# Down projection on one core: side blocks of weights loaded later in the lead, and the next sum's first operand rounded ahead of the current sum's second pass

## The chip, the cores and the metric

The kernel runs on one core of one Trainium2 chip, in one launch. The metric is device time in microseconds (us). Three runs of the kernel before gave 2108.65, 2109.05 and 2110.7 us; their median is 2109.05 us. One more execution was profiled: it took 2109.45 us, and its span, from the first to the last instruction of the program, is 2107.5 us.

## The reference, cut to what matters

Two layers of a decoder trunk in float32, on x of 512 tokens by 1024. Each layer has two feed-forward modules (with a mixer of recurrence and attention between them), so there are four feed-forward modules in all:

```
def swiglu(h, w_gate, w_up, w_down):
    return (jax.nn.silu(h @ w_gate) * (h @ w_up)) @ w_down     # D = 1024, D_FF = 2816

x = x + 0.5 * rms_norm(swiglu(rms_norm(x, gn[0]), w_ffn1_gate[l], w_ffn1_up[l], w_ffn1_down[l]), gn[1])
...
x = x + 0.5 * rms_norm(swiglu(rms_norm(x, gn[4]), w_ffn2_gate[l], w_ffn2_up[l], w_ffn2_down[l]), gn[5])
```

The change touches the last product of each feed-forward module, the activations (512 x 2816) by `w_down` (2816 x 1024): the down projection.

## The kernel before, in words

**Every product is three matmuls.** A float32 operand is split into a rounded part (hi, type float32r) and what is left (lo). `mm3` (L211) multiplies hi by hi, hi by lo and lo by hi. So each operand costs ScalarE one copy for hi and VectorE one subtraction for lo (`split`, L230); in `split_dma` (L241) ScalarE makes hi and minus the source (lines L408 and L409 of the profile), and GpSimd issues a DMA that adds the source (L410). For weights the copies are L274 and L322.

**Engines and order.** TensorE's order is the order of the code. The instructions of the other engines are ordered when the program is built, by a scheduler that follows the code where nothing is in the way; `pin` keeps an instruction behind the one written before it on its engine. Once built, each engine runs its own queue in order, and waits on semaphores.

**Tiles.** `big()` (L52) gives a 2 KB per partition tile of the pool tag `s`, which has 61 rooms (`SLOTS`). Tiles of one tag get their rooms in the order in which the code first writes them, and each takes the free room that has been free longest; the writer then waits on the chip until the last reader of the room's old tile is done. Weights arrive in four `w32` tiles; their hi and lo parts live in six `whi` and six `wlo` tiles.

**The down projection (`down`, `fast=True`).** The activations are 22 blocks `src[k]` of 128 features by 512 tokens. The first 12 go through a product of seven quarter products (`quarters`), the last 10 through ordinary products. It runs in this order:

1. The **lead**: five units j = 6 to 10 (`both(j, 0)`), each with the blocks k = 2j and 2j+1, four token blocks and three matmuls each: 24 matmuls of 512 columns. The blocks 16 to 21 are rounded into `part` just ahead of it, 12 tiles of `s`; the tiles of a unit come free when the unit is done.
2. During the lead `Late.sums` (L615) makes the operands of the quarter products, one call for each k = 0 to 5, two calls after each of the first three units. A call splits the first half of `src[k]` into `x1[k]` (ScalarE copy L398, VectorE L399), builds sums `s` and `t` (VectorE L456, L457, L459, L460), and splits `t` by `split_dma` into `x37` (L408, L409, L410). It takes five tiles of `s`.
3. The seven products in the order p1, p3, p7, p2, p6, p4, p5 (`ORDER`), each of 36 matmuls: six k, two token blocks, three matmuls. Each uses three blocks of weights, q = 0 to 2, made in `Stream.quarter`. p1 uses the raw blocks; p3 and p5 the side blocks `b22`; p7 the side blocks `b12` after `b22` has been added to them (L255).
4. The second half of the ordinary products, and the norm.

**Order of the weights.** `Stream` holds the blocks of weights in the order in which TensorE uses them. A used block leads to the splits of the blocks ahead (`ahead`, with `most` of them), and a split block lets `load` issue the next DMA on SyncE's queue (SP; L233 and L236). In `load`, when the last raw block of p1 has been asked for, the 24 DMAs of the side blocks follow on the same queue at once (L245): two tiles of `s` for each of three q, for `b22` and for `b12`, 12 tiles in all. This is ahead of the lead in the code. After `whi` of p1's block q = 0, which is written in the third unit, those of q = 1 and 2 are written in the fourth unit, that is behind all six sums, and they are pinned there.

Of the kernel before, what the change touches and what calls it, by code (L numbers as in the profile page):

```python
# [8 lines left out]
F32R = mybir.dt.float32r  # L9
# [6 lines left out]
P = 128  # L16
D = 1024
S = 512
# [14 lines left out]
    first=0.0, spread=2300.0, squares=1700.0, lay=34500.0, laid=770.0, normed=7600.0, final=2600.0,  # L33
# [11 lines left out]
def trunk(ctx: ExitStack, tc: tile.TileContext, xin, wall, gains, lbT, hgain, sinks, c_dist, c_mask, c_ident, out):  # L45
    nc = tc.nc
    cp = ctx.enter_context(tc.tile_pool(name="cp", bufs=1))
    sb = ctx.enter_context(tc.tile_pool(name="sb", bufs=1))
    ps = ctx.enter_context(tc.tile_pool(name="ps", bufs=1, space=PSUM))
# [8 lines left out]
    def nm(s):  # L58
        seq[0] += 1
        return f"{s}_{seq[0]}"  # L60

    def big(dt=F32, shape=None):
        return sb.tile(shape or [P, S], dt, tag="s", name=nm("s"), bufs=SLOTS)
# [15 lines left out]
    class Order:  # L79
        def __init__(self):  # L80
            self.t = 0.0
            self.rest = 0.0
            self.cos = []
# [60 lines left out]
    pin = tc.keep_in_program_order  # L144
# [10 lines left out]
    class Stream:  # L155
        def __init__(self):
            self.n, self.wall = 0, 0
            self.items = []
            self.raw, self.dma = {}, 0
            self.done, self.flight = 0, 0  # L160
            self.cur, self.c = 0, 0
            self.src = {}
            self.pinned = False
            self.most = AHEAD
            self.side, self.freed = {}, 0

        def plain(self, n, kind="u"):
            self.items += [Item(kind, self.n + i) for i in range(n)]
# [23 lines left out]
        def rows(self, kt, fast):  # L192

            u0 = self.wall

            def pieces(j, h):
                b = [(4 * h + i) * kt + 2 * j for i in range(4)]
                return [(slice(i * 2 * P, (i + 1) * 2 * P), wall[u0 + n // 8][:, n % 8 * P : (n % 8 + 2) * P]) for i, n in enumerate(b)]  # L200

            def unit(j, h):
                c = 2 * j * P
                self.src[self.n] = [(None, wall[u0 + 4 * h : u0 + 4 * h + 4, :, c : c + 2 * P].rearrange("u p c -> p u c"))] if kt == 8 else pieces(j, h)
                self.plain(1)

            lead = range(SEVEN // 2 if fast else 0, kt // 2)
            for j in lead:
                unit(j, 0)
            if fast:  # L210

                u, n = self.n, SEVEN // 4
                for q in range(n):
                    self.src[u + q] = pieces(q, 0)
                    self.src[u + n + q] = pieces(n + q, 0)
                self.side[u + n - 1] = [pieces(n + q, 1) for q in range(n)], [pieces(q, 1) for q in range(n)]
                for k in ORDER:
                    for q in range(n):
                        it = Item(k, u + q + (n if k in ("p2", "p4") else 0), 4)
                        it.base, it.q = u, q  # L220
                        self.items.append(it)
                self.n += 2 * n
            for j in lead:
                unit(j, 1)
            self.wall = u0 + kt

        def load(self, upto):
            while self.dma < min(upto, self.n):
                w = sb.tile([P, D], F32, tag="w32", name=nm("w32"), bufs=W32)
                u = self.dma  # L230
                if isinstance(self.src[u], list):
                    for c, a in self.src[u]:
                        nc.sync.dma_start(w.rearrange("p (m c) -> p m c", m=4) if c is None else w[:, c], a)  # L233
                else:
                    for c in (slice(0, D // 2), slice(D // 2, D)) if u == 0 else (slice(0, D),):
                        nc.sync.dma_start(w[:, c], wall[self.src[u]][:, c])  # L236
                self.raw[u] = w
                self.dma += 1
                if u in self.side:
                    self.b22, self.b12, self.t2 = [], [], []  # L240
                    for b, side in zip((self.b22, self.b12), self.side[u]):  # L241
                        for ps in side:
                            v = [big(), big()]
                            for c, a in ps:
                                nc.sync.dma_start(v[c.start // S][:, c.start % S : c.start % S + 2 * P], a)  # L245
                            b.append(v)

        def quarter(self, it):

# [42 lines left out]
        def split(self):  # L292
            it = self.items[self.done]
            if it.kind[0] == "p":
                return self.quarter(it)
            u, last = it.u, it.kind in "uvd"
            self.load(u + (1 if it.kind in "uv" else 2))
            it.hi = sb.tile([P, D], F32R, tag="whi", name=nm("whi"), bufs=WS)
            it.lo = sb.tile([P, D], F32R, tag="wlo", name=nm("wlo"), bufs=WS)
            w, h = self.raw[u], (slice(0, D // 2), slice(D // 2, D))  # L300
            cols = (slice(0, D),)
            if it.kind == "u" and u == 0:
                cols = h
            if it.kind in "bcd":
                v = self.raw[u + 1]
            if it.kind == "b":

                self.t13 = sb.tile([P, D], F32, tag="tt", name=nm("tt"), bufs=2)
                pin(nc.vector.tensor_tensor(self.t13[:, h[0]], w[:, h[0]], v[:, h[0]], op=ALU.add))
                pin(nc.vector.tensor_tensor(self.t13[:, h[1]], v[:, h[0]], v[:, h[1]], op=ALU.add))  # L310
                w = self.t13
            elif it.kind == "c":

                t = sb.tile([P, D], F32, tag="tt", name=nm("tt"), bufs=2)
                pin(nc.vector.tensor_tensor(t[:, h[0]], self.t13[:, h[0]], v[:, h[1]], op=ALU.add))
                pin(nc.vector.tensor_tensor(t[:, h[1]], t[:, h[0]], w[:, h[1]], op=ALU.add))  # L316
                w = t
            elif it.kind == "d":
                w = v
                cols = h[1:]  # L320
            for c in cols:
                i = nc.scalar.copy(it.hi[:, c], w[:, c])  # L322
                if u < 3 or self.pinned:
                    pin(i)
                if it.kind in "vad":
                    nc.scalar.mul(it.lo[:, c], w[:, c], -1.0)  # L326
                    nc.gpsimd.dma_start(it.lo[:, c].bitcast(F32), w[:, c], accum_op=ALU.add)  # L327
                else:
                    nc.vector.tensor_tensor(it.lo[:, c], w[:, c], it.hi[:, c].bitcast(F32), op=ALU.subtract)  # L329
            self.done += 1  # L330
            self.flight += 1
            if last:
                nu = u + (1 if it.kind in "uv" else 2)
                for i in range(u, nu):
                    self.raw.pop(i)
                    self.freed += 1
                self.load(self.freed + W32)
# [38 lines left out]
    ws = Stream()  # L376
# [37 lines left out]
    HALF = (slice(0, S // 2), slice(S // 2, S))  # L414
# [51 lines left out]
    def pair_split(v, how=split):  # L466
        return how(v, to=(big(F32R, [P, 2, S // 2]), big(F32R, [P, 2, S // 2])))
# [139 lines left out]
    class Late(Quarters):  # L607
# [5 lines left out]


        def sums(self):  # L615
            k = len(self.x1)
            a = [self.src[i][:, c] for i in (k, k + self.n) for c in HALF]
            x = big(F32R, [P, 2, S // 2])
            self.x1.append(split(a[0], to=(x[:, 0, :], x[:, 1, :]), hold=pin))
            s, t = quarter_sums(a[0], a[2], a[1], a[3], True)  # L620
            self.s.append(s)
            self.x37.append(pair_split(t, split_dma))
            self.src[k] = ()

        def rest(self):
            for k in range(self.n, 2 * self.n):
                self.src[k] = split_dma(self.src[k])
# [9 lines left out]
    def down(src, kt, l, n, nxt, fast):  # L637
# [47 lines left out]

        if fast:
            late = Late(src)
            ws.pinned = True
            for k in range(2 * js[0] + EARLY, kt):
                part[k] = split(src[k], hold=pin)  # L690
            for i, j in enumerate(js):
                ws.most = (3, 2, 2, 3, 3)[i]
                both(j, 0)
                while len(late.x1) < min(late.n, 2 * i + 2):
                    late.sums()
                for k in (2 * j, 2 * j + 1):
                    part.pop(k, None)
            ws.pinned = False
            more = quarters(late, y, lambda: (ready(kt), fetch()))
        else:  # L700
            for j in js:
                ready(2 * j + 2 + EARLY)
                both(j, 0)
            fetch()
# [762 lines left out]
```

## Time and profile before

| what | value |
|---|---|
| median of three runs | 2109.05 us |
| the profiled execution, its own time | 2109.45 us |
| its span | 2107.5 us |
| TensorE matmul busy | 2087.7 us, 99% |
| VectorE busy | 1588.2 us, 75% |
| ScalarE busy | 1180.9 us, 56% |
| DMA, mean over the span | 149 GB/s |
| share of the granted TensorE clock, mean | 0.996 |

Times inside the trace are counted from the start of the span. The first feed-forward module has its lead at about 241 to 268 us; the other three have the same work at about 938, 1285 and 1980 us. In a row of the timeline stand the start, the length, the engine, the line, the operation with its tiles (out<-in), the shape, how often, and in brackets the idle time of the engine just before and what ended it. The lines that carry the argument are shown in the prediction.

### The profile page before, as it was taken

To read this page: it belongs to the slowest core of one execution; us is meant where nothing else is said; L and a number is where in the kernel's file an instruction comes from. 1 tells how busy PE (TensorE), PEld (TensorE's weight loads), DVE (VectorE), ACT (ScalarE), POOL (GpSimd) and SP (SyncE) were. 2 spreads that over 40 slices of the span, in tenths; PEclk is the share of its full clock that TensorE was granted. 3 is DMA by queue.
4 is the path that set the end of the run, shared out by engine and by line. 5 is a ranking of instruction groups with operands and counts; after the bars stand their busy time and mean duration, and the time that the engine had idled before them with its cause. 6 is when DMAs were issued, how large, how long until landed. Compare 5 with 4: busy or idle time off the path is not lost. (4 is left out here: it accounts for less than half of the span.)

```text
span 2107.5 us, 35599 instructions
## 1 busy us (share of the span) xinstructions
PE 2087.7 (99%) x13501; PEld 1870.3 (89%) x13501; DVE 1588.2 (75%) x2801; ACT 1180.9 (56%) x2035; POOL 203.1 (10%) x244
## 2 busy tenths in 40 slices
PE   9999999999999999999999999999999999999998
PEld 8899978887888999997899998888778989999977
DVE  5877779766786777786987777887686758777777
ACT  6555566456454555556555555754654545555564
POOL 0011120000000011112001111100000000111120
PEclk9999999999999999999999999999999999999999
DMA  8577865312236357776637777652122563677863
GB/s 247 151 182 182 215 126 194 111 61 71 71 101 203 127 122 182 183 198 150 189 112 175 182 182 194 140 193 93 51 81 60 136 194 101 163 181 182 213 135 108
DMA packets 156139, 313.07 MB, mean 149 GB/s; under 512 B 17888, under 2 KB 75712, under 8 KB 155968
## 3 DMA queue, kind: packets, MB, share of 16 engines
q1 hardware_dynamic: 122416, 228.16, 32.9%
q0 software_dynamic: 33408, 82.59, 22.7%
q8 instruction: 106, 1.74, 0.3%
q14 instruction: 65, 0.53, 0.1%
q10 hardware_dynamic: 144, 0.05, 0.0%
HBM read 213.43 MB, written 14.73 MB: 108 GB/s over the span
## 5 line engine op out<-in xcount | busy, mean ns | idle before, releaser
L114 PE MATMUL acc<-s,whi 128*128 128x256 f32 (+1 forms) x4952 | 1059.9, 311 | 0.6 <-ACT whi L322 0.4
L114 PEld LDWEIGHTS acc<-s,whi 128*128 128x128 f32 x4952 | 808.0, 191 | 52.4 <-issue 4.0
L114 PE MATMUL acc<-s,wlo 128*128 128x256 f32 (+1 forms) x2476 | 766.5, 310 | 0.1
L114 PEld LDWEIGHTS acc<-s,wlo 128*128 128x128 f32 x2476 | 472.6, 191 | 24.9 <-DVE wlo L329 0.4
L114 PE MATMUL acc<-whi,s 128*128 128x512 f32 x1344 | 442.3, 396 | 9.8 <-ACT whi L274 9.8
L322 ACT CAST whi<-w 128x512 fp32r<-128x512 f32 (+1 forms) x325 | 299.6, 942 | 163.0 <-PE acc L114 107.5
L322 ACT CAST whi<-tt 128x1024 fp32r<-128x1024 f32 x154 | 161.4, 1048 | 327.2 <-DVE tt L316 188.5
L114 PEld LDWEIGHTS acc<-whi,s 128*128 128x128 f32 x1344 | 254.4, 189 | 69.4 <-ACT whi L274 11.5
L329 DVE TENSOR_TENSOR wlo<-w,whi 128x1024 fp32r<-128x1024 f32 (+1 forms) x165 | 199.8, 1215 | 89.6 <-ACT whi L322 88.9
L114 PE MATMUL acc<-wlo,s 128*128 128x512 f32 x672 | 264.4, 393 | 1.2 <-DVE wlo L277 1.2
L329 DVE TENSOR_TENSOR wlo<-tt,whi 128x1024 fp32r<-128x1024 f32 x154 | 188.1, 1222 | 99.8 <-ACT whi L322 99.5
L327 POOL DMA_DIRECT2D wlo<-w x160 | 138.2, 864 | 1231.2 <-ACT wlo L326 715.5
L114 PE MATMUL aux<-s,whi 128*128 128x256 f32 (+1 forms) x1248 | 230.4, 285 | 0.0
L114 PEld LDWEIGHTS aux<-s,whi 128*128 128x128 f32 x1248 | 195.2, 192 | 1.1 <-issue 0.5
L114 PE MATMUL aux<-s,wlo 128*128 128x256 f32 (+1 forms) x624 | 177.5, 284 | 0.0
L114 PE MATMUL aux<-whi,s 128*128 128x512 f32 x480 | 159.2, 390 | 0.0
L114 PEld LDWEIGHTS acc<-wlo,s 128*128 128x128 f32 x672 | 127.5, 190 | 27.5 <-DVE wlo L277 2.5
L326 ACT ACTIVATE wlo<-w 128x1024 fp32r<-128x1024 f32 (+1 forms) x160 | 129.8, 844 | 0.0
L114 PEld LDWEIGHTS aux<-s,wlo 128*128 128x128 f32 x624 | 119.8, 192 | 0.3
L114 PEld LDWEIGHTS aux<-whi,s 128*128 128x128 f32 x480 | 90.1, 188 | 18.6
L911 DVE SCALAR_TENSOR_TENSOR s<-m 128x512 f32<-128x512 f32 x69 | 47.8, 693 | 76.2 <-ACT m L910 75.7
L398 ACT CAST s<-s 128x512 fp32r<-128x512 f32 (+1 forms) x148 | 78.2, 563 | 47.2 <-DVE s L457 43.6
(185 smaller groups left out, 2374.4 us busy)
## 6 DMA issues: line engine op xcount, KB each, us to landing
w<-wall SPq DMA_DIRECT2D x267, 512.0 KB, 3.8
wlo<-w POOLq DMA_DIRECT2D x83, 512.0 KB, 5.5
w<-wall SPq DMA_DIRECT2D x256, 128.0 KB, 3.1
wlo<-w POOLq DMA_DIRECT2D x77, 256.0 KB, 3.3
s<-s POOLq DMA_DIRECT2D x72, 256.0 KB, 4.8
x_d<-s SPq DMA_DIRECT2D x48, 256.0 KB, 2.1
s<-wall SPq DMA_DIRECT2D x96, 128.0 KB, 3.5
s<-x_d SPq DMA_DIRECT2D x48, 256.0 KB, 5.3
```

The lines of the kernel that those rows point to most:

```text
L114: nc.tensor.matmul(o, lhsT, rhs, start=start, stop=stop)
L322: i = nc.scalar.copy(it.hi[:, c], w[:, c])
L326: nc.scalar.mul(it.lo[:, c], w[:, c], -1.0)
L327: nc.gpsimd.dma_start(it.lo[:, c].bitcast(F32), w[:, c], accum_op=ALU.add)
L329: nc.vector.tensor_tensor(it.lo[:, c], w[:, c], it.hi[:, c].bitcast(F32), op=ALU.subtract)
L398: hold(nc.scalar.copy(hi, src))
L911: nc.vector.scalar_tensor_tensor(z, m[:, 0:2, :], -1.0, m[:, 2:4, :], op0=ALU.mult, op1=ALU.mult)
```

## The change

The side blocks are no longer loaded in `load`. A new function `aside` issues the same DMAs into the same kind of tiles; `down` calls it for `b22` after the third unit of the lead and its sums (`i == 2`), and for `b12` after the fourth unit (`i == 3`). `Late.sums` is turned: the split of the first operand moves into a function `first`; the call for k makes its sums, then calls `first(k + 1)`, and then splits `t`. Instructions and DMAs are the same in number, size and kind; only their places differ.

```
     def rows(self, kt, fast):
-                self.side[u + n - 1] = [pieces(n + q, 1) for q in range(n)], [pieces(q, 1) for q in range(n)]
+                self.side.append(([pieces(n + q, 1) for q in range(n)], [pieces(q, 1) for q in range(n)]))
     def load(self, upto):
-                if u in self.side:
-                    self.b22, self.b12, self.t2 = [], [], []
-                    for b, side in zip((self.b22, self.b12), self.side[u]):
-                        for ps in side:
-                            v = [big(), big()]
-                            for c, a in ps:
-                                nc.sync.dma_start(v[c.start // S][:, c.start % S : c.start % S + 2 * P], a)
-                            b.append(v)
+        def aside(self, pieces):
+            b = []
+            for ps in pieces:
+                v = [big(), big()]
+                for c, a in ps:
+                    nc.sync.dma_start(v[c.start // S][:, c.start % S : c.start % S + 2 * P], a)
+                b.append(v)
+            return b
     def sums(self):                                   # class Late
-            k = len(self.x1)
+            k = len(self.s)
             a = [self.src[i][:, c] for i in (k, k + self.n) for c in HALF]
-            x = big(F32R, [P, 2, S // 2])
-            self.x1.append(split(a[0], to=(x[:, 0, :], x[:, 1, :]), hold=pin))
+            if not k:
+                self.first(0)
             s, t = quarter_sums(a[0], a[2], a[1], a[3], True)
             self.s.append(s)
+            if k + 1 < self.n:
+                self.first(k + 1)
             self.x37.append(pair_split(t, split_dma))
             self.src[k] = ()
+        def first(self, k):
+            x = big(F32R, [P, 2, S // 2])
+            self.x1.append(split(self.src[k][:, HALF[0]], to=(x[:, 0, :], x[:, 1, :]), hold=pin))
     def down(...):
             late = Late(src)
+            b22, b12 = ws.side.pop(0)
...
                 both(j, 0)
-                while len(late.x1) < min(late.n, 2 * i + 2):
+                while len(late.s) < min(late.n, 2 * i + 2):
                     late.sums()
+                if i == 2:
+                    ws.b22 = ws.aside(b22)
+                elif i == 3:
+                    ws.b12, ws.t2 = ws.aside(b12), []
```

More of the change, by code (lines that the diff above doesn't have):

```diff
@@ L164, in __init__ @@
             self.most = AHEAD
-            self.side, self.freed = {}, 0
+            self.side, self.freed = [], 0
         def plain(self, n, kind="u"):
```

## The prediction

> **What bounds the kernel now.** The page comes first:
>
> ```profile
> span 2107.5 us, 35599 instructions
> ...
> PE 2087.7 (99%) x13501; PEld 1870.3 (89%) x13501; DVE 1588.2 (75%) x2801; ACT 1180.9 (56%) x2035; POOL 203.1 (10%) x244
> ```
>
> TensorE (PE) is busy for all but 19.8 us. The change removes no matmul, so it can only win what TensorE waits. The waits of TensorE alone:
>
> ```profile
> PE acc L114 <- ACT whi L274: 9.8, 4, 2.4
> ...
> PE acc L114 <- DVE wlo L277: 1.2, 4, 0.3
> ```
>
> L274 and L277 make hi and lo of the weights of the quarter products. TensorE waits for them once in each of the four feed-forward modules: 2.45 us for hi, 0.3 for lo. The timeline of TensorE at the first of these places:
>
> ```profile
> 268.25 0.39 PE L114 MATMUL acc<-whi,s 128*128 128x512 f32 x1
> ...
> 270.52 0.39 PE L114 MATMUL acc<-wlo,s 128*128 128x512 f32 x1
> 270.75 0.39 PE L114 MATMUL acc<-whi,s 128*128 128x512 f32 x1
> 273.58 0.50 PE L114 MATMUL acc<-whi,s 128*128 128x512 f32 x1 [2.44 <-ACT whi L274]
> 274.39 0.50 PE L114 MATMUL acc<-wlo,s 128*128 128x512 f32 x1 [0.31 <-DVE wlo L277]
> 274.73 0.85 PE L114 MATMUL acc<-whi,s 128*128 128x512 f32 x2
> 275.37 0.63 PE L114 MATMUL acc<-wlo,s 128*128 128x512 f32 x1
> 275.80 1.05 PE L114 MATMUL acc<-whi,s 128*128 128x512 f32 x2
> 276.65 0.63 PE L114 MATMUL acc<-wlo,s 128*128 128x512 f32 x1
> 277.08 1.05 PE L114 MATMUL acc<-whi,s 128*128 128x512 f32 x2
> 277.93 0.60 PE L114 MATMUL acc<-wlo,s 128*128 128x512 f32 x1
> 278.36 0.64 PE L114 MATMUL acc<-whi,s 128*128 128x512 f32 x2
> 278.84 0.40 PE L114 MATMUL acc<-wlo,s 128*128 128x512 f32 x1
> ```
>
> p1's first matmul starts at 268.25, where the lead ends, and its twelfth, the last of block q = 0, at 270.75: a step is 2.50 / 11 = 0.227 us. The place costs more than the idle time in brackets. From 270.75 to 274.73 there are 3 steps, worth 0.68 us, and they take 3.98: 3.30 us lost. From 274.73 to 278.84 there are 11 steps, worth 2.50, and they take 4.11: 1.61 us more, with no wait at all. The windows say why; they are the 10 us ahead of the first place, and 5 us behind each of the four:
>
> ```profile
> 260.00:270.00 10.00, 10.00 (x46) 8.29 (x45) 5.25 (x13) 3.99 (x9) 1.72 (x2) 1.00 0.64 146
> ...
> 273.50:278.50 5.00, 4.61 (x12) 3.43 (x13) 5.00 (x10) 4.19 (x9) 0.15 (x1) 0.66 0.30 52
> 970.00:975.00 5.00, 4.63 (x12) 3.46 (x13) 5.00 (x10) 4.16 (x9) 0.13 (x1) 0.66 0.31 54
> 1317.00:1322.00 5.00, 4.69 (x20) 3.65 (x20) 5.00 (x9) 3.93 (x8) 0.00 (x0) 1.00 0.32 56
> 2012.00:2017.00 5.00, 4.69 (x14) 3.50 (x15) 5.00 (x10) 3.99 (x8) 0.86 (x1) 0.66 0.30 52
> ```
>
> The column after the brackets is the granted clock: 1.00 ahead, 0.66 behind three of the four waits. So three places cost 3.30 + 1.61 = 4.91 us and the third, where the clock stays, 3.30: together 3 x 4.91 + 3.30 = **18.0 us**.
>
> **Why hi comes late.** A unit is 24 x 0.227 = 5.45 us; the lead ends at 268.25, so its units 3, 4 and 5 end at 257.4, 262.8 and 268.25. VectorE and ScalarE in that time:
>
> ```profile
> 256.67 0.43 DVE L456 TENSOR_TENSOR s<-s,s 128x256 f32<-128x256 f32 x1 [1.18 <-PE aux L114]
> 257.01 0.42 DVE L460 TENSOR_TENSOR s<-s 128x256 f32<-128x256 f32 x1
> ...
> 262.11 0.42 DVE L460 TENSOR_TENSOR s<-s 128x256 f32<-128x256 f32 x1 [3.21 <-PE aux L114]
> ...
> 273.04 1.29 DVE L277 TENSOR_TENSOR wlo<-w,whi 128x512 fp32r<-128x512 f32 x2 [1.72 <-ACT whi L274]
> ```
>
> ```profile
> 263.75 0.62 ACT L408 CAST s<-s 128x512 fp32r<-128x512 f32 x1 [3.63 <-DVE s L459]
> ...
> 264.81 1.12 ACT L274 CAST whi<-w 128x512 fp32r<-128x512 f32 x2
> ...
> 268.62 0.62 ACT L408 CAST s<-s 128x512 fp32r<-128x512 f32 x1 [2.38 <-issue]
> ...
> 271.35 0.62 ACT L408 CAST s<-s 128x512 fp32r<-128x512 f32 x1 [1.28 <-DVE s L459]
> ...
> 272.41 2.16 ACT L274 CAST whi<-w 128x512 fp32r<-128x512 f32 x4
> ```
>
> The sums for k = 2 and k = 3 wait for TensorE (1.18 and 3.21 us). L456 and L460 read only activations that were finished long before, so what they wait for is the room of the tile that they write: a `part` tile of unit 3 and of unit 4, each just before the unit's end. The chain then runs without slack: 262.11 is when the room comes free, the L408 of k = 3, 4 and 5 follow at 263.75, 268.62 and 271.35, and the hi of block q = 1, pinned behind them, at 272.41. TensorE wanted it one step behind 270.75, at 270.98.
>
> **The change part by part.** It adds and removes no instruction and no DMA.
>
> *Side blocks later.* The 12 tiles of `s` are now asked for behind the sums. Rooms go out in code order, oldest free room first, so `part` and the first sums move up by 12 rooms in that queue. The sums k = 0 to 3 then need none of the rooms that wait for units 3 and 4; those for k = 4 and 5 get rooms of earlier sums and of unit 3, free at 257.4. The waits of 1.18 and 3.21 us go. SyncE's queue:
>
> ```profile
> 245.66 12.64 SPq L245 DMA_DIRECT2D s<-wall  x24
> 258.40 3.07 SPq L233 DMA_DIRECT2D w<-wall  x4
> ```
>
> ```profile
> DMA to landing us min/median/max: 2.2/3.5/6.2
> ```
>
> The second row is of the L245 DMAs. An issue takes 12.64 / 24 = 0.53 us. On this queue the side DMAs move behind one raw block, p2's first (258.40), which is no longer held up; nothing else stands behind them until p7 frees a raw block. By my count of the rooms `b22` gets them from 257.4 on, the last at about 262, and `b12` right after, the last at about 267. Then the first block of `b22` lands at about 257.4 + 4 x 0.53 + 3.5 = 263 and its last at 268; TensorE wants p3 at 268.3 + 36 x 0.227 = 276.4. The first block of `b12` is the 16th DMA: 257.4 + 8.5 + 3.5 = 269.4, a little later with the rooms; p7 comes at 284.6. So I cost the later loads at nothing; what hides them is p1 and p3, 16.3 us of matmuls.
>
> *First operand ahead.* The rhythm of the sums, where no room was missing, is that of k = 0 and 1:
>
> ```profile
> 252.78 0.62 ACT L408 CAST s<-s 128x512 fp32r<-128x512 f32 x1 [2.87 <-DVE s L459]
> ...
> 253.84 0.39 ACT L398 CAST s<-s 128x256 fp32r<-128x256 f32 x1
> 255.57 0.62 ACT L408 CAST s<-s 128x512 fp32r<-128x512 f32 x1 [1.34 <-DVE s L459]
> ```
>
> A sum takes 255.57 - 252.78 = 2.79 us, as L398 of the next stands behind L408 and L409 on ScalarE and VectorE's work behind L398. With L398 a call ahead the two engines no longer take turns. The bounds: 2.79 us if nothing comes of it, and five VectorE steps at 0.34 us (256.67, 257.01), 1.7 us, if VectorE is never kept waiting. I take 1.8, since ScalarE then needs about 1.6. The copies of q = 0 (264.81 to the next instruction, about 1.06) stand between k = 3 and 4. The last L408 then starts at 252.78 + 5 x 1.8 + 1.06 = 262.8, and the copies of q = 1 at 263.9; with 2.79 they start at 268.9. Copies to finished lo took 274.33 - 272.41 = 1.92 us, so lo is there at 265.8 or at 270.8, before 270.98 either way: the wait is gone at both ends, by 5 us or by nearly nothing.
>
> **Sum.** The profiled execution of 2109.45 us less 18.0 gives 2091.4; the median of the runs, 2109.05, is 0.4 lower, so **2091.0 us**, 0.86% faster. What is late next shows at the other end of the quarter products; VectorE at p7's first sum and p4's last lo, and TensorE's use of it:
>
> ```profile
> 279.07 1.29 DVE L255 TENSOR_TENSOR s<-s,s 128x512 f32<-128x512 f32 x2
> ```
>
> ```profile
> 318.63 0.68 DVE L277 TENSOR_TENSOR wlo<-w,whi 128x512 fp32r<-128x512 f32 x1
> ```
>
> ```profile
> 319.67 0.39 PE L114 MATMUL acc<-wlo,s 128*128 128x512 f32 x1
> ```
>
> lo is done at 319.31 and read at 319.67, a slack of 0.36 us. With TensorE 4.91 us earlier, the chain from p7 on must be that much earlier too. It should be: VectorE runs without a gap from 273.04 to 279.07 on blocks that now start some 5 to 8 us sooner, and what follows also hangs on the copies of p1's result, which move with TensorE.
>
> **Rivals.**
>
> *Side blocks too late (slower).* If their rooms come free only when unit 5 ends (268.3), p7's first sum waits for 268.3 + 16 x 0.53 + 3.5 = 280.3. It has to start by 279.07 - 4.91 + 0.36 = 274.5, and each us beyond is lost in each module: 5.8 x 4 = 23 us against 18.0, so 2114 us. It turns the sign from a first sum at 279.0 on. Against it: 12 `part` tiles come free before that, and the six `t` tiles.
>
> *The rooms go as before (no change).* DMAs that read only weights wait for nothing but rooms and could still be placed ahead of the sums; then 3.21 us stays and the time is 2109. Against it: rooms go out in code order, and the code now puts the sums first.
>
> *Given back behind p1.* If the chain to p4 moves by only half of 4.91 in each module, 4 x 2.1 = 8 us come back: 2099; in one module alone, 2093.
>
> *The half clock stays.* If the slow stretches are not the waits' doing, the sum is 4 x 3.30 = 13.2, and the time 2095.8. The rows speak against it: 1.00 before, 0.66 straight behind three waits of equal length. [...]
>
> **How the numbers follow.** My forecast 0.65 (2089 to 2093); given back 0.12 (2093 to 2102); half clock stays 0.04; no change 0.06; slower 0.13 (2110 to 2119). A measurement tells 0.2% (4.2 us) from no change. Faster is 0.65 + 0.12 + 0.04 = 0.81, same 0.06, slower 0.13. The range 2089 to 2102 holds the first three. Its lower end leaves 2 us of the 8.8 that TensorE idles elsewhere (19.8 - 9.8 - 1.2).
>
> **What the profile after would show.** If right: no TensorE wait on L274 or L277; granted clock 1.00 behind p1; no VectorE wait on PE at L456 or L460 of the lead; L408 about 1.8 us apart; L245 from about 257 on; L255 before 274.5. If the waits stay at L274 while those of L456 and L460 are gone, the rhythm was mis-sized; if a wait stands at p3 or p7 instead, the loads; if at p6 or p4, the chain behind p1.

## The result, and the profile after

Five runs of each kernel: 2109.59 us before (2108.65 to 2110.7) and **2090.30 us** after (2090.12 to 2092.28), a ratio of 0.9911 (95% interval 0.9896 to 0.9925). The prediction was 2091.0 us. The profiled execution of the changed kernel took 2091.05 us, 18.4 less than that of before.

In the changed file the lines have moved: L410 and L411 are before's L408 and L409, L458 to L462 its L456 to L460, L276 and L279 its L274 and L277, L246 its L245, and L257 its L255. The first part of the page:

```profile
span 2089.3 us, 35596 instructions
...
PE 2080.3 (100%) x13501; PEld 1866.8 (89%) x13501; DVE 1588.0 (76%) x2801; ACT 1182.6 (57%) x2035; POOL 203.1 (10%) x244
```

TensorE now idles for 9.0 us (2089.3 - 2080.3) and not 19.8. Its waits over the whole program, as the view lists them:

```profile
PE acc L124 <- DVE s L756: 2.9, 1, 2.9
PE aux L114 <- DVE eps_t L137: 1.1, 1, 1.1
PE acc L114 <- DVE s L501: 0.3, 1, 0.3
```

No wait for the weights of the quarter products is left. The windows just behind the start of p1 in the four modules, with the granted clock in the third column from the right:

```profile
270.00:275.00 5.00, 5.00 (x24) 4.13 (x23) 3.79 (x7) 1.87 (x3) 0.00 (x0) 1.00 0.85 245
962.00:967.00 5.00, 5.00 (x24) 4.14 (x23) 3.87 (x7) 1.76 (x3) 0.00 (x0) 1.00 0.84 234
1305.00:1310.00 5.00, 5.00 (x24) 4.14 (x23) 3.08 (x6) 1.24 (x2) 0.00 (x0) 1.00 0.70 200
1995.00:2000.00 5.00, 5.00 (x24) 4.14 (x23) 3.07 (x5) 1.87 (x3) 0.00 (x0) 1.00 0.94 258
```

TensorE is busy throughout (the number behind the length of the window, 5.00 of 5.00) and the clock stays at 1.00. Next ScalarE in the first lead, then VectorE, then SyncE's queue, then TensorE:

```profile
253.36 0.62 ACT L410 CAST s<-s 128x512 fp32r<-128x512 f32 x1 [2.50 <-DVE s L461]
...
255.16 0.62 ACT L410 CAST s<-s 128x512 fp32r<-128x512 f32 x1 [0.35 <-DVE s L461]
...
256.96 0.62 ACT L410 CAST s<-s 128x512 fp32r<-128x512 f32 x1 [0.35 <-DVE s L461]
...
258.76 0.62 ACT L410 CAST s<-s 128x512 fp32r<-128x512 f32 x1 [0.35 <-DVE s L461]
...
263.63 0.62 ACT L410 CAST s<-s 128x512 fp32r<-128x512 f32 x1 [1.33 <-issue]
...
264.69 2.17 ACT L276 CAST whi<-w 128x512 fp32r<-128x512 f32 x4
```

```profile
255.38 0.42 DVE L458 TENSOR_TENSOR s<-s,s 128x256 f32<-128x256 f32 x1
...
257.51 0.42 DVE L462 TENSOR_TENSOR s<-s 128x256 f32<-128x256 f32 x1
257.85 0.42 DVE L459 SCALAR_TENSOR_TENSOR s<-s,s 128x256 f32<-128x256 f32 x1
258.30 0.43 DVE L461 TENSOR_TENSOR s<-s,s 128x256 f32<-128x256 f32 x1
...
265.33 2.50 DVE L279 TENSOR_TENSOR wlo<-w,whi 128x512 fp32r<-128x512 f32 x4 [1.77 <-ACT whi L276]
...
271.99 0.69 DVE L257 TENSOR_TENSOR s<-s,s 128x512 f32<-128x512 f32 x1
273.25 0.69 DVE L257 TENSOR_TENSOR s<-s,s 128x512 f32<-128x512 f32 x1 [0.58 <-DMA s<-wall]
```

```profile
257.28 16.45 SPq L246 DMA_DIRECT2D s<-wall  x24
```

```profile
268.65 0.39 PE L114 MATMUL acc<-whi,s 128*128 128x512 f32 x1
...
271.59 0.39 PE L114 MATMUL acc<-wlo,s 128*128 128x512 f32 x1
```

The sums for k = 2 and 3 (255.38 and 257.51) no longer wait for TensorE; they waited 1.18 and 3.21 us. The second passes follow each other at 1.80 us. Hi of block q = 1 starts at 264.69 and not at 272.41; its lo is done by about 266.6 and is read at 271.59, 5 us later. The side DMAs go out from 257.28 on. One load of p7 comes late without harm: the second sum of p7 waits 0.58 us for it, and no TensorE wait follows.

**Where the time came from.** Both traces hold the same 13,501 matmuls in the same order, so the start of each can be set against the start of the same one in the other trace. Over p1 and p3 the kernel before loses 4.95, 4.93, 3.32 and 4.77 us against the changed one in the four modules, 17.97 in all; behind p3 it loses 0.21 in the third module and 0.0 in the others. By the last matmul the difference is 18.3 us: at the end of the program before loses 0.6 more, and in the first 28 us it had gained 0.4.

### The profile page after: what moved, and what is told of

The parts are those of the page before. It is cut to its first block, busy times and chain, and to the rows that moved or that the text cites. A ratio compares the mean times of both kernels' runs of the same rounds, so it can differ in the third digit from the quotient of the medians.

```text
span 2089.3 us, 35596 instructions
## 1 busy us (share of the span) xinstructions
PE 2080.3 (100%) x13501; PEld 1866.8 (89%) x13501; DVE 1588.0 (76%) x2801; ACT 1182.6 (57%) x2035; POOL 203.1 (10%) x244
## 4 chain that ended last, share of the span: by engine, by line
PE 98%; DMA 1%; ACT 0%; DVE 0%; SPq 0%; issue 0%
PE acc L114 74%; PE aux L114 23%; PE aux L124 1%; PE acc L124 1%; DMA s<-xin 0%; DMA w<-wall 0%; DMA g_sb<-gains 0%; ACT s L500 0%; ACT whi L324 0%; DVE s L756 0%; DVE s L501 0%; ACT s L430 0%; ACT s L599 0%; DVE s L737 0%; DVE s L431 0%
## 5 line engine op out<-in xcount | busy, mean ns | idle before, releaser
L114 PE MATMUL acc<-whi,s 128*128 128x512 f32 x1344 | 437.7, 393 | 0.0
L329 POOL DMA_DIRECT2D wlo<-w x160 | 138.2, 863 | 1234.0 <-ACT wlo L328 732.9
```

What stands on the lines that cost most here:

```text
L114: nc.tensor.matmul(o, lhsT, rhs, start=start, stop=stop)
```

## The experiments

**The theory**: rooms handed out in code order held the sums back, the lead then ended ahead of block q = 1, and three of the four waits cost a stretch of half clock as well. **The rivals**: only the order of the sums counts; the loads themselves held the sums back; the loads become the limit once they are late.

Lines shift by a few from kernel to kernel: L259, L278 and L281 in e6 and e9 are before's L255, L274 and L277, and L730 in e2 and L731 in e1 are before's L724. The table has one row for each kernel but e4 and e8, which bring the waits back for a question about the clock. Its first entry for a module is the start of p7's first sum, in us behind p1's first matmul; then what TensorE loses against the changed kernel over p1 and p3, and behind p3, the second half of the ordinary products included.

```
                      module 1          module 2          module 3          module 4
before               10.81 4.95 0.00   10.82 4.93 0.00   10.82 3.32 0.21   10.82 4.77 0.00
changed               3.34 0.00 0.00    3.38 0.00 0.00    3.38 0.00 0.00    4.74 0.00 0.00
e1 side blocks only   8.18 0.67 1.05    8.03 0.55 0.24    7.90 0.43 1.07    8.63 1.14 0.50
e2 order only         8.33 0.87 2.60    8.33 0.85 1.78    8.33 0.87 1.72    8.33 0.87 1.61
e3 before, 62 rooms   9.29 1.79 1.11    9.28 1.79 0.07    9.28 1.79 0.47    9.29 1.81 0.03
e5 delay of 4.5 us    6.73 0.00 1.08    6.56 0.00 0.08    6.64 0.00 0.33    7.62 0.14 0.88
e6 b12 later          5.74 0.00 0.93    6.04 0.00 0.07    5.89 0.00 0.00    5.49 0.00 0.00
e7 54 rooms           6.87 0.00 1.48    6.27 0.00 0.62    6.48 0.00 0.03    8.07 0.00 1.93
e9 b12 behind p1     11.65 0.00 4.75   11.58 0.00 3.95   11.44 0.00 4.14   11.58 0.00 3.84
e10 b22 early         2.89 0.00 0.23    2.89 0.00 0.00    2.97 0.00 0.00    3.09 0.00 0.00
```

### The side blocks alone (e1)

The changed kernel with the old `sums`:

```
-            if not k:
-                self.first(0)
+            x = big(F32R, [P, 2, S // 2])
+            self.x1.append(split(a[0], to=(x[:, 0, :], x[:, 1, :]), hold=pin))
             s, t = quarter_sums(a[0], a[2], a[1], a[3], True)
             self.s.append(s)
-            if k + 1 < self.n:
-                self.first(k + 1)
...
```

> Only the side blocks move; the sums keep their old order. If rooms are what held the sums of k = 2 and 3 (theory), no wait on TensorE is left at the first sum's two tiles (it was 1.18 and 3.21 us), the L410 of the sums follow each other in about 2.8 us, the copies of block q = 1 start at about 268.9 and its lo is there at about 270.8, just when TensorE wants it: at most 0.5 us of waiting in each lead, 2090 to 2093 us. If the order of the sums is what counts (rival), the late hi stays and the time is above 2105.

Measured: 2097.04 us, ratio to before 0.9943 (0.9929 to 0.9956). ScalarE, and then TensorE at p1 and behind p5:

```profile
265.67 0.62 ACT L410 CAST s<-s 128x512 fp32r<-128x512 f32 x1 [2.39 <-DVE s L461]
268.46 0.62 ACT L410 CAST s<-s 128x512 fp32r<-128x512 f32 x1 [1.34 <-DVE s L461]
269.52 2.16 ACT L276 CAST whi<-w 128x512 fp32r<-128x512 f32 x4
```

```profile
271.51 0.50 PE L114 MATMUL acc<-wlo,s 128*128 128x512 f32 x1 [0.30 <-DVE wlo L279]
...
329.43 0.50 PE L114 MATMUL acc<-whi,s 128*128 128x512 f32 x1 [0.35 <-DVE s L731]
```

The mechanism at p1 came as expected: the passes 2.79 us apart, the copies of q = 1 at 269.52, a wait of 0.3 us there (0.2 in the second module, none over 0.15 in the third, 0.3 for hi and 0.3 for lo in the fourth). The time did not: 4 us more than the 2093 at the top of the range. By the table 2.8 us are lost at p1 over the four modules and 2.9 behind p3, some of it in waits for L731, the VectorE sum that reads out an `acc` tile which TensorE writes next.

### The order of the sums alone (e2)

The kernel before with the new `sums` and `first`, and the loads of `load` left as they were.

> Only the rounding of the next first operand goes ahead; the side blocks are loaded ahead of the lead as before, so the rooms stay short: the waits on TensorE of the sums of k = 2 and 3 (about 1.2 and 3.2 us) should be there again, and the second pass of k = 3 starts at about 263.7 as before. From there the faster rhythm gives 1.8 us for each of two sums and 1.06 for the copies of q = 0: the copies of q = 1 start at about 269.3, hi is there in time and lo at about 271.2, within 0.5 us of the want. Theory (both parts shorten one chain that was only 2.5 us late, so either is enough): 2091 to 2096. Rival (while rooms are short the order wins nothing): 2109.

Measured: 2102.03 us, 0.9964 (0.9952 to 0.9977). VectorE:

```profile
256.88 0.42 DVE L456 TENSOR_TENSOR s<-s,s 128x256 f32<-128x256 f32 x1 [1.65 <-PE aux L114]
...
262.32 0.42 DVE L460 TENSOR_TENSOR s<-s 128x256 f32<-128x256 f32 x1 [3.21 <-PE aux L114]
```

The waits for rooms are back, 1.65 and 3.21 us, and yet 7.4 us are won: at p1 only 0.87 is lost in each module. But 7.7 us are lost behind p3, which the expectation did not count; the time is 6 us above its range. TensorE at the place that recurs in all four modules:

```profile
331.78 0.39 PE L114 MATMUL acc<-whi,s 128*128 128x512 f32 x1
333.01 0.50 PE L114 MATMUL acc<-whi,s 128*128 128x512 f32 x1 [0.85 <-DVE s L730]
```

Together e1 and e2 win 12.4 + 7.4 = 19.8 us, and the whole change 19.3: each part is needed, and neither is enough.

### One room more (e3)

```
-SLOTS = 61
+SLOTS = 62
```

> The kernel before with one room more (62), all else as before. If rooms in a fixed order are the cause (theory), every request moves up by one room: the sums of k = 3 no longer wait for unit 4, only the second pass of k = 3 does, and can start when unit 4 gives up its first tile, at about 262.1 and not at 263.75. The copies of q = 1 come 1.6 us earlier, the wait for hi falls from 2.45 to about 0.8 us, and with at most one stretch of half clock left the time is 2096 to 2101. If the loads of the side blocks hold the sums up by traffic or by their queue (rival), one room changes nothing: 2109.

Measured: 2102.07 us, 0.9965 (0.9952 to 0.9979). ScalarE at the second pass of k = 3, and TensorE's waits:

```profile
261.92 0.62 ACT L408 CAST s<-s 128x512 fp32r<-128x512 f32 x1 [2.39 <-PE aux L114]
```

```profile
PE acc L114 <- ACT whi L274: 3.7, 4, 0.9
```

One 2 KB room, with loads and order as before, takes the wait for hi from 2.45 to 0.9 us and wins 7 us; the pass that started at 263.75 starts at 261.92. That the requests move up in a fixed order of rooms is shown by this; the loads, which are all where they were, do not explain it, and e10 puts half of them back without a loss at p1. A kernel with all loads early and rooms for all of them was not run. The time is 1 us above the range.

### Block q = 1 delayed (e4, e5, e8)

Idle copies on ScalarE behind the last sum of each lead, as many as a list `DELAY` says for the four leads (9, 12, 14 and 17 in e4, 7 in each in e5, 11, 12, 12 and 11 in e8):

```
             self.x37.append(pair_split(t, split_dma))
+            if k + 1 == self.n:
+                junk = sb.tile([P, S], F32, tag="junk", name=nm("junk"), bufs=1)
+                for _ in range(DELAY.pop(0)):
+                    pin(nc.scalar.copy(junk, s.rearrange("p a b -> p (a b)")))
```

> The changed kernel, with 9, 12, 14 and 17 idle copies of 0.52 us put on ScalarE behind the last sum of the first, second, third and fourth lead: 4.7, 6.2, 7.3 and 8.8 us of delay for block q = 1. By the change's own trace hi is there some 5.6 us ahead of TensorE, so the first lead should lose nothing, the others wait about 0.6, 1.7 and 3.2 us. Theory for the clock (a grid of 3.413 us stretches that runs by itself; a stretch in which TensorE idles for more than about 2 us halves the clock in the next): half clock behind the fourth, not behind the second, behind the third only if the wait falls inside one stretch; the starts of slow stretches in the trace are whole multiples of 3.4133 us apart; 2099 to 2102 us. [...]

Measured (one run): 2114.96 us. A copy took 0.64 us and not 0.52, so the delays were 5.8, 7.7, 9.0 and 10.9 us, and TensorE waited for hi 0, 1.82, 2.88 and 5.69 us. A stretch of 3.41 us at a granted clock of 0.50 followed each of the second and third wait (from 968.69 and 1316.85), and two the fourth (from 2013.17). The numbers expected were therefore missed, and "not behind the second" with them. In the first module TensorE waits 0.3 us at p1 and still loses 2.4 behind p3.

> The changed kernel with 7 idle ScalarE copies of 0.64 us behind the last sum of every lead: block q = 1 of p1 is 4.5 us later, about as late as with the side blocks alone moved (4.8 us), but the loads, the rooms and the order of the sums are those of the change. The changed kernel's slack at p1 is 4.6 us for the latest lo, so no wait over 0.2 us is due at p1. Theory (what the side blocks alone fail to win is the lateness of VectorE's chain from p1 to the end of the quarter products, handed on to TensorE later): small waits of TensorE at the products behind p7 or at the sums behind p5, most of them in the third and fourth module, where the changed kernel has the least slack, 2093 to 2098 us, near the 2097.0 of that run. Rival (the loss there came from the order of the sums or from the loads, not from lateness): 2090 to 2091.

Measured: 2093.68 us, 0.9923 (0.9911 to 0.9936). At p1 0.14 us are lost, behind p3 2.4, against 2.9 in e1: lateness alone, with loads and order as in the changed kernel, gives back nearly as much behind p3 as e1 does. The time lies in the lower part of the range, and the modules do not fit it: the first loses most (1.08), and the third and fourth lose 0.33 and 0.88, where e1 loses 1.07 and 0.50. By the table p7's first sum is some 1.3 us less late here than in e1, so the two are not quite of one size.

> The changed kernel with 11, 12, 12 and 11 idle ScalarE copies of 0.64 us in the four leads: waits of TensorE for hi of about 1.2 to 1.9 us, and 0.3 more for lo. Theory for the clock: on a grid of 3.4133 us stretches, a stretch with less than 1.7 us of idle time is followed by a full clock and one with more than 2.1 us by a half one (those were the largest idle time without and the smallest with a slow stretch so far); the starts of all slow stretches lie on one grid. [...]

Measured (one run): 2110.3 us, with waits for hi of 1.04, 1.89, 1.70 and 1.71 us. The windows are laid in steps of 3.4133 us from the start of its slow stretch at 1316.10; TensorE's busy time is the number behind the length of the window:

```profile
967.94:971.36 3.42, 2.22 (x8) 1.61 (x9) 3.06 (x6) 3.42 (x8) 0.00 (x0) 1.00 0.59 176
971.36:974.77 3.41, 3.41 (x16) 2.81 (x15) 3.41 (x7) 1.81 (x5) 0.00 (x0) 1.00 0.02 7
1312.69:1316.10 3.41, 1.41 (x6) 0.62 (x5) 1.71 (x3) 3.38 (x7) 0.00 (x0) 1.00 0.88 263
1316.10:1319.52 3.42, 3.42 (x10) 2.65 (x9) 3.42 (x7) 2.94 (x6) 0.00 (x0) 0.50 0.19 61
...
2009.01:2012.42 3.41, 1.72 (x8) 1.10 (x6) 0.52 (x1) 3.31 (x7) 0.00 (x0) 1.00 0.99 261
2012.42:2015.84 3.42, 3.10 (x12) 2.36 (x13) 3.42 (x7) 3.42 (x7) 0.00 (x0) 1.00 0.75 229
```

Of the waits of nearly one size in the second, third and fourth module only that of the third was followed by a clock of 0.50: its stretch (1312.69) held the 1.70 us and the 0.3 us wait for lo, 2.00 in all. That of the second fell into two stretches (1.20 us of idle time, lo included, in the part shown), and in the fourth 1.69 us fell into one stretch; behind both the clock was 1.00. As expected, then; the last section takes it up.

### The loads later (e6, e9), fewer rooms (e7), only b12 late (e10)

e6 and e9 put a small GpSimd copy into each tile of `b12`, which its DMAs must wait for. In e6 it reads hi of p3's last block; in e9 it reads p1's result, and until then fewer blocks of weights are split ahead (`most` is 2):

```
                 v = [big(), big()]
+                for d in v if after is not None else ():
+                    nc.gpsimd.tensor_copy(d[:, :1], after)
```

> The changed kernel with b12 not asked for until hi of p3's last block is made (a small GpSimd copy into each of its tiles holds the loads back): the DMAs of b12 go out from about 271.5 and not from 263, the first sum of p7 starts at about 277 and not at 272. Theory (the slower rival of the prediction: from a point on, every us of lateness of p7's first sum is a us of TensorE): the slack of the changed kernel behind p7 is 1.6 to 4.2 us by module, so 1 to 3.5 us are lost in each, 2098 to 2106 us. Rival (the loads are hidden by p1 and p3 however late they are asked for, as the prediction costs them): 2090 to 2091.

Measured: 2091.86 us, 0.9913 (0.9898 to 0.9928). VectorE at p7's first sum:

```profile
273.90 0.69 DVE L259 TENSOR_TENSOR s<-s,s 128x512 f32<-128x512 f32 x1 [2.42 <-DMA s<-wall]
```

The sum started 2.4 us behind the expected issue of the loads (271.5), not 5.5. So the dose was 2 us and not 5; it cost 0.93 us in the first module and next to nothing elsewhere. The expected range was missed because the landing was over-estimated: the GpSimd copies that hold the loads back started at 270.81, and the sum that needs the first load started 3.1 us later. The rival's range was missed by 0.9 us, and the run tells little.

> The changed kernel with the loads of b12 held back until p1's result has been copied out (small GpSimd copies into their tiles, which wait for that copy): the DMAs start at about 277, the first block lands at about 282.7 and p7's first sum starts there, 10.7 us later than with the change. Theory (the slower rival of the prediction): the changed kernel has 2 to 4 us of slack behind it, VectorE's line from there to the end of the quarter products is later by the rest, and TensorE waits for it in every module, 5 to 8 us each: 2112 to 2125 us, slower than the kernel before. Rival (the work behind p7 catches up, since VectorE is busy for only three quarters of the time): below 2100.

Measured: 2108.17 us, 0.9992 (0.9983 to 1.0002): the whole gain is gone, and no more. VectorE at p7's first sum, and TensorE at p7's second block:

```profile
280.20 1.32 DVE L259 TENSOR_TENSOR s<-s,s 128x512 f32<-128x512 f32 x2 [7.77 <-DMA s<-wall]
```

```profile
287.37 0.39 PE L114 MATMUL acc<-whi,s 128*128 128x512 f32 x1
289.19 0.50 PE L114 MATMUL acc<-whi,s 128*128 128x512 f32 x1 [1.43 <-ACT whi L278]
290.00 0.50 PE L114 MATMUL acc<-wlo,s 128*128 128x512 f32 x1 [0.31 <-DVE wlo L281]
```

The loads can become the limit: 3.8 to 4.8 us a module, nearly all at p7 itself and not at p4 (in the third module a stretch at a granted clock of 0.50, from 1333.32, is part of it). Both sides of the expectation were missed, 2112 and above as well as below 2100.

e7 is the changed kernel with `SLOTS = 54`.

> The changed kernel with 54 rooms and not 61. By the order of the rooms b22 then waits for unit 4 (262.8) and b12 for unit 5 (268.3): the first sum of p7 starts at about 275, some 3 us later than with the change. Theory: the first lead loses nothing (3.3 us of slack), the third and fourth lose 1 to 2 us each, 2092 to 2097 us, unless other stages need the seven rooms too, which would show as waits outside the four down projections. Rival (rooms do not matter once the side blocks are asked for late): 2090 to 2091.

Measured: 2101.61 us, 0.9958 (0.9944 to 0.9972). In the down projections 4.1 us are lost, about as much as expected, but not where: the first module loses 1.48 and the third 0.03. The rest is in stages without a down projection, with these waits among them:

```profile
PE aux L114 <- ACT s L1086: 3.7, 2, 1.9
```

e10 is the changed kernel with `ws.b22 = ws.aside(b22)` ahead of the lead again.

> The changed kernel with b22 loaded ahead of the lead again, and only b12 late. By the order of the rooms the sums of k = 0 to 4 still need nothing that unit 4 gives up; only the second tile of k = 5 waits for it (about 262), when its first pass would be due anyway at about 262. Theory (only six of the twelve rooms are needed): the copies of q = 1 start within 1 us of the changed kernel's 264.7, no wait at p1, 2090 to 2092 us. Rival (both have to move): half of the old waits come back, 2093 to 2100.

Measured: 2090.71 us, 0.9907 (0.9892 to 0.9922), the same as the whole change. ScalarE:

```profile
264.34 2.17 ACT L276 CAST whi<-w 128x512 fp32r<-128x512 f32 x4
```

Six of the twelve rooms are enough; that `b22` moves as well brings nothing.

## Why the prediction was right, point by point

- **The sum.** 4.91 us at three places and 3.30 at the third, 18.0 in all, was the term; 4.95, 4.93, 3.32 and 4.77 came back. The first 3.30 of each is made up of waits of 2.44 and 0.31 us and 0.55 more at the matmuls around them, the other 1.6 the stretch at a granted clock of 0.50. Median to median 19.3 us went, 1.3 more than the sum; the two medians of before, 2109.05 of three runs and 2109.59 of five, already differ by 0.5.
- **Rooms.** Shown by e3 and by the two waits that vanish with the change and return in e2.
- **The rhythm.** 1.8 us was chosen between 1.7 and 2.79, and 1.80 came. VectorE is never kept waiting, and one of its five steps takes 0.45 us (257.85 to 258.30) and not 0.34; the reason given, ScalarE's 1.6 us, set only a bound, so that the choice came out to the digit is luck. The copies of q = 1 were put at 263.9 and started at 264.69, as the last sum's VectorE work stood behind the lo of q = 0.
- **The loads at nothing.** Right: they started at 257.28 (257.4 said), and p7's first sum, due by 274.5, started at 271.99. The 24 issues took 16.45 us and not 12.64, and the last of `b22` came later than said (ScalarE waited for it until 270.7, 268 was said) without harm.
- **The order "by 5 us or by nearly nothing".** This step did not bear on the forecast, but it was wrong. It said that at a rhythm of 2.79 us the wait is gone as well, and so let the order cost nothing. In e1 the passes are 2.79 us apart and the waits at p1 are 0.3 us or less each, and yet e1 is 6.7 us slower than the whole change: 2.8 us are lost at p1 and 2.9 behind p3. So the 5 us ahead are not idle reserve. What needs them is, as far as e5 shows it (2.4 us lost behind p3 by lateness alone), VectorE's line from p1's lo through p7's sums and p4's lo to the sums behind p5. The prediction had this as a rival (given back behind p1) and not as a condition of its forecast.
- **The slower rival.** Its point was about right: 274.5 is 6.25 us behind p1's first matmul, and in the rows of the table without a loss at p1, losses behind p3 set in between 5.7 and 6.9, in some modules and not in others (0.93 at 5.74 and 0.03 at 6.48), but for 0.23 in e10's first module. Its price, one for one, was too high: e9's first sum started at 280.20 (280.3 was said), 4.2 us a module were lost and not 5.8, and the time was that of before, not 2114.

**Left open.** Counted from the end of the wait at p1, p7's first sum is about 7.5 us late in e1, e2 and e3 alike, but e2 loses 7.7 us behind p3, e1 2.9 and e3 1.7. One piece can be seen: VectorE has no gap there, and in e2 five L329 and six L399 of later work stand between the products' last lo and the second L730, in the kernel before four and four (L724 there). The scheduler fixes that order when the program is built. Why it comes out so was not tried.

## What to carry to other kernels

The sums of k = 2 and 3 waited 1.18 and 3.21 us for TensorE when all their operands had long been there; these were waits for the room of their output: what is asked for early and used late (here loads) took rooms from what is used soon, and one room more was a cheap test of it (e3: the wait for hi went from 2.45 to 0.9 us). When a wait at one engine is removed, look at the busiest other engine behind it: how far ahead its chain has to be decides how much of the gain stays, and a version that removes most of the wait can win a third less: e1 won 12.4 of 19.3 us. Price a wait of TensorE with what follows it: a wait of 2.45 us, with 0.3 behind it, cost 3.3 us alone and 4.9 with a stretch at a clock of 0.50 behind it.

## What the runs showed of the hardware

**Where the granted clock was halved.** In before's trace it falls from 1.00 to 0.50 at 274.97, 971.29 and 2012.35, for 3.41 us each time (and once more at 2101.10, at the end of the program); the three starts are 204 and 305 times 3.4133 us apart. In the traces of before and after every change of the granted clock lies within 0.004 us of whole multiples of 3.4133 us from the others of its trace, and e4's slow stretches from 968.69, 1316.85 and 2013.17 are 102 and 204 times 3.4133 us apart. Before's first and third place, whose waits have one length:

```profile
271.56:274.97 3.41, 1.08 (x4) 0.68 (x5) 1.93 (x4) 3.41 (x7) 0.86 (x1) 1.00 0.66 115
274.97:278.38 3.41, 3.41 (x10) 2.64 (x9) 3.41 (x6) 2.72 (x6) 0.00 (x0) 0.50 0.20 34
...
1312.62:1316.04 3.42, 1.75 (x8) 1.13 (x6) 1.18 (x3) 2.14 (x5) 0.88 (x2) 1.00 0.43 75
1316.04:1319.45 3.41, 2.33 (x9) 1.72 (x10) 3.18 (x6) 3.41 (x8) 0.85 (x1) 1.00 0.48 83
```

At the first TensorE idles for 2.33 us in one stretch, and the next has 0.50. At the third the idle time falls into two stretches, 1.67 us in one and 1.08 in the other, and the clock stays at 1.00. The closest pair is in e7, at two waits of 1.86 us:

```profile
570.72:574.13 3.41, 1.73 (x11) 1.38 (x9) 2.50 (x6) 1.60 (x3) 0.00 (x0) 1.00 0.00 0
574.13:577.54 3.41, 3.23 (x21) 2.98 (x22) 0.64 (x1) 1.87 (x4) 0.00 (x0) 1.00 0.00 0
1608.37:1611.78 3.41, 1.55 (x14) 1.36 (x13) 1.57 (x3) 1.54 (x3) 0.00 (x0) 1.00 0.00 0
1611.78:1615.20 3.42, 3.42 (x15) 3.03 (x14) 0.69 (x1) 2.06 (x3) 0.00 (x0) 0.50 0.02 5
```

Idle for 1.68 of 3.41 us the clock stayed at 1.00; idle for 1.86 it was 0.50 in the next stretch. In the traces of before and after, and in the stretches with these waits in e3, e4, e7, e8 and e9, leaving out the end of the program, 1.69 us was the largest idle time in a stretch without a slow one behind it (e8, fourth module) and 1.86 the smallest with one (e7); none of them lies between the two. This is for stretches at full clock: at the end of the program before's stretch from 2101.10, at half clock itself and idle for 1.47 us, was followed by half clock again. Waits of 1.82 us (e4, second module) and 1.70 us (e8, third), each with 0.3 behind it in the same stretch, and of 1.86 us alone (e7) were followed by a clock of 0.50.
